# Second layer's long filters made during the first layer's merges and kept in DRAM; the step between the layers in two parts of the tokens

## The chip, the cores and the metric

One core of a Trainium2 chip. The time is that of one execution on the device in microseconds (us); the kernel before takes 2286.52 us, median of three runs (2286.14 to 2286.73). PE multiplies matrices, DVE works on vectors, ACT on activations and casts, POOL and SP also issue DMA transfers. All engines run their own instruction list in order and wait for each other by semaphores.

## The reference

Two layers over 128 context tokens and 512 latent tokens (640 columns, "T"), model width 1024. Each layer is one mixer with four branches from one input projection, gated, merged and projected:

```python
for l in range(DEPTH):                                   # DEPTH = 2
    shift, scale, gate = split(silu(cond) @ w_ada + b_ada, 3)
    h = rms_norm(x, norm_g) * (1.0 + scale) + shift
    u = h @ w_in                                          # 1024 -> 10752 columns in all
    ya = conformer_conv(...)  @ wo_conv                   # conv over 31 tokens
    filt = hyena_filters(L, ...)                          # depends on weights alone
    yb = hyena(u_proj, ..., filt, skip) @ wo_hyena        # long conv through FFT
    yc = multiscale_pool(...) @ wo_pool
    yd = block_attention(...) @ wo_attn
    gm = sigmoid(g_merge)                                 # one gate per branch
    merged = gm[0]*ya + gm[1]*yb + gm[2]*yc + gm[3]*yd
    x = x + gate * (merged @ w_out)
```

The filters come from a small network over the token position, are multiplied by a decay, normed and transformed (`spectra`); they need nothing of x.

## The kernel before

All matrices are held as a high and a low part of a 32-bit number, so a projection of 1024 rows into 128 columns over 640 tokens is, for each half j of 320 tokens, 16 matmuls with the high weights (`whi`) and 8 with the low (`wlo`), each 320 columns wide (`proj`, L386). A weight comes by a chain: SP loads `raw` (2 buffers), ACT casts `whi`, ACT writes −`whi` into `wlo`, POOL adds the original to it by an accumulating DMA (3 pairs of `whi`/`wlo`). Big data lie in 13 slots of SBUF (`sl`); projections use three PSUM banks (`mm`), small work three (`ax`), the transform one (`sc`).

The order on PE is planned when the program is built: `Loom` (L84) runs generators, its threads, each with a priority, and a thread yields the time from which it could go on; PE's order is what the planner chose. The other engines are ordered by the framework's scheduler, which follows what is ready and its priorities.

The stages of a layer: convolution stage with filters of the Hyena branch (`Hyena`, L839) and the branch's inputs, v/k/q, attention together with the Hyena branch's merge (`first`, written to `mscr`), the conformer's and pooling's inputs, then three merges of eight steps d each (attention, pooling, conformer; `merge`, L805), then `out_proj` (L1771): four blocks n of 256 output columns in token-major form, five tiles of 128 tokens, 24 matmuls each (`token_proj`, L418). Each block adds to the residual x, stores it (`store_x`), sums the squares of x and spawns `turned` (L752), which transposes x for the next layer and multiplies by 1 + scale. In between the chunks of w_ada for the next layer's shift and scale are done (`ada_chunk`, L603). After all four blocks `rms` (L712) makes the norm's factors from the sums, and `modulated` (L773) does, per 128 rows k of the eight: DVE's product with the factors (`u`), ACT's high part, DVE's low part. A projection of the next layer waits k by k on `a.ev[k]`.

A filter thread (`filters`, L872; one for each half q, four pieces c each) fetches decay (320 KB) and `hy_w` (64 KB) into the slot of the piece, casts the weights into `k` on ACT, does 10 matmuls `ax<-k,hd`, squares and sums, two tiny matmuls `ax<-ones`, and the transform: 8 matmuls into `sc`, 6 into `ax`, which DVE folds into the slot (`wx`, then `sl<-wx`). The second layer's eight pieces are spawned by `late_filters` (L1905) in the second block of out_proj (`ev_late`, L1779), so that they lie in out_proj, the step between the layers and the second layer's first projections.

Of the kernel before, what the change touches and what calls it, by code (L numbers as in the profile page):

```python
# [16 lines left out]
P = 128  # L17
# [215 lines left out]
def hybrid_flow_backbone(ctx: ExitStack, tc: tile.TileContext, i, o):  # L233
# [179 lines left out]
    def in_proj(l, c0, fn):  # L413
        w = yield from w_cols(l, c0)
        yield from both(w, 0, hT[0], 8, fn)
        wr.put(WD)

# [70 lines left out]
    scratch = tc.dram_tile([T, D], F32, name="xscratch")  # L488
    dve.memset(lnw, 1.0 / 512.0)
# [205 lines left out]
    def square_sum(xs, ssq, n):  # L695
        h, c0 = n // 2, 256 * (n % 2)
        for t in range(5):
# [14 lines left out]
    def rms(ssq):  # L712
        v = sm.tile([P, 5], F32, tag="rmsv", name=nm("rmsv"))
        rs = sm.tile([P, 5], F32, tag="rmsr", name=nm("rmsr"))
        dve.tensor_reduce(out=v, in_=ssq, axis=AX.X, op=ALU.add)
        dve.tensor_scalar(out=v, in0=v, scalar1=1.0 / D, scalar2=EPS, op0=ALU.mult, op1=ALU.add)
        rsqrt(rs, v, 5)
        return rs

    def modulated_first(a, xs, ssq):  # L720

        rs = rms(ssq)
        for h in range(2):
            xv = xs[h].v(0, 5, 512)
            for t in range(5):
                dve.tensor_scalar(out=xv[:, t, :], in0=xv[:, t, :], scalar1=rs[:, t:t + 1], scalar2=None,
                                  op0=ALU.mult)
        for h in range(2):
            xv = xs[h].v(0, 5, 512)
            yield lm.sync()  # L730
            pp = yield from ax.get()
            for c in range(4):
                pe.transpose(pp[:, 128 * c:128 * c + 128], xv[:, 0, 128 * c:128 * c + 128], ident)
            for c in range(4):
                k = 4 * h + c
                yield ev_mod[0][k // 2]
                ps = yield from mm.get()
                for t in range(4):
                    pe.transpose(ps[:, 128 * t:128 * t + 128], xv[:, 1 + t, 128 * c:128 * c + 128], ident)
                hf = yield from tr.get(T)  # L740
                A, S = mods[0][:, 1, k, :], mods[0][:, 0, k, :]
# [6 lines left out]
                a.ev[k].set()  # L748
            ax.put()
            xs[h].free()  # L750

    def turned(l, xs, xT, n, ev):  # L752
# [5 lines left out]
        for u in range(2):  # L758
# [3 lines left out]
            for t in range(4):  # L762
                pe.transpose(ps[:, 128 * t:128 * t + 128], xv[:, 1 + t, c], ident)
            A = mods[l][:, 1, 2 * n + u, :]
            act.activation(out=dst[:, 128:640], in_=ps, func=AF.Copy, scale=A[:, 1:2])
            mm.put()
            pp = yield from ax.get()
            pe.transpose(pp[:, 0:128], xv[:, 0, c], ident)
            act.activation(out=dst[:, 0:128], in_=pp[:, 0:128], func=AF.Copy, scale=A[:, 0:1])
            ax.put()  # L770
        ev.set()

    def modulated(l, a, xT, ssq, evs):  # L773

        rs = rms(ssq)
        yield lm.sync()
        row = yield from tr.get(T)
        ps = yield from mm.get()
        for t in range(1, 5):
            pe.transpose(ps[:, 128 * t - 128:128 * t], rs[:, t:t + 1].to_broadcast([P, P]), ident)  # L780
        act.copy(row[:, 128:640], ps)
        mm.put()
        pp = yield from ax.get()
        pe.transpose(pp[:, 0:128], rs[:, 0:1].to_broadcast([P, P]), ident)
        act.copy(row[:, 0:128], pp[:, 0:128])
        ax.put()
        for k in range(8):
            yield evs[k // 2]
            x = xT[k // 4].v((k % 4) * T, T)
            hf = yield from ur.get(T)  # L790
            S = mods[l][:, 0, k, :]
            dve.tensor_tensor(out=hf, in0=x, in1=row, op=ALU.mult)
            for c, t in ((1, slice(128, 640)), (0, slice(0, 128))):
                hi, lo, f = a.h(k)[:, t], a.l(k)[:, t], hf[:, t]
                act.activation(out=hi, in_=f, func=AF.Identity, bias=S[:, c:c + 1])
                dve.scalar_tensor_tensor(out=lo, in0=f, scalar=S[:, c:c + 1], in1=r32(hi),
                                         op0=ALU.add, op1=ALU.subtract)
            ur.put()
            a.ev[k].set()
            if k % 4 == 3:  # L800
                xT[k // 4].free()
# [37 lines left out]
    class Hyena:  # L839
# [32 lines left out]
        def filters(self, q):  # L872

            l = self.l
            if q == 0 and l > 0:
                s = yield from slot()
                self.tables(s)
# [27 lines left out]
            for c in range(4):  # L905
                if q == 0 and c not in self.flt:
# [3 lines left out]
                self.fetch(c, q)  # L910
                yield self.ld[c, q]
# [3 lines left out]
                if c < 3 and q == 0 and c + 1 not in self.flt and free and (self.gB or c < 1):  # L915
                    self.flt[c + 1] = Slot()
                if c + 1 in self.flt:
                    self.fetch(c + 1, q)
# [53 lines left out]
                self.ev_f[c, q].set()  # L972
            self.nf += 1
            if self.nf == 2:
                self.Bf.free()

# [47 lines left out]
        def inputs(self, c):  # L1024
# [4 lines left out]
            for u in range(3):  # L1029
# [4 lines left out]
                def take(j, ps):  # L1034
# [3 lines left out]
                    else:  # L1038
                        act.copy(pad[:, 322:642], ps)

                yield from in_proj(l, C_BP + 512 * u + 128 * c, take)
                uc = s.v(641 * u, 641)
                act.activation(out=uc, in_=pad[:, 1:642], func=AF.Identity,
                               scale=par(l, c, R_SW + 3 + u), bias=par(l, c, R_SB + u))
                for k in (0, 2):
                    dve.scalar_tensor_tensor(out=uc, in0=pad[:, k:k + 641],
                                             scalar=par(l, c, R_SW + 3 * k + u), in1=uc,
                                             op0=ALU.mult, op1=ALU.add)
                tr.put()
# [721 lines left out]
    def out_proj(l, ma, xs, ssq, rows, xT=None, evs=None):  # L1771
        for n in range(4):
# [6 lines left out]
            if n == 1:  # L1779
                ev_late[l].set()  # L1780
# [3 lines left out]
            def take(t0, ps):  # L1784
# [6 lines left out]
                tr.put()  # L1791

            yield from token_proj(i["w_out"][l][:, 256 * n:256 * n + 256], ma, take)
# [3 lines left out]
            else:  # L1797
                store_x(xs, scratch[0:LP], scratch[LP:T], n)
                square_sum(xs, ssq, n)
                lm.spawn(turned(l + 1, xs, xT, n, evs[n]), PT)  # L1800

    def layers():
# [3 lines left out]
        xT, evs = None, None  # L1806
        for l in range(DEPTH):
            hy = hys[l]
            a = yield from new_act(2)
            a.ev = [Event(lm) for _ in range(8)]  # L1810
            lm.spawn(modulated(l, a, xT, ssq, evs) if l else modulated_first(a, xs, ssq), PN)
# [10 lines left out]
            hy.gB = yield from slot()  # L1822
            at = Attention(l)
# [40 lines left out]
            yield from po.gated()  # L1864
            yield from merge(l, 2, po.pa, 4, i["wo_pool"][l], merged, "mid")
# [3 lines left out]
            ma = yield from new_act(2)  # L1869
# [12 lines left out]
            if l + 1 < DEPTH:  # L1882
                lm.spawn(late_filters(l + 1, ev_late[l]), 7)
                lm.spawn(ada_later([(1, j) for j in range(8, 12)], 0.0, GS), 50, LATA)
            if l + 1 < DEPTH:
                xT = yield from slots(2)
                evs = [Event(lm) for _ in range(4)]
            yield from out_proj(l, ma, xs, ssq, rows, xT, evs)
# [3 lines left out]
            if l + 1 < DEPTH:  # L1892
                yield evs[3]
# [11 lines left out]
    def late_filters(l, ev):  # L1905
        yield ev
        for q in range(2):
            hys[l].threads.append(lm.spawn(hys[l].filters(q), PF0))

# [4 lines left out]
    ev_late = [Event(lm) for _ in range(DEPTH)]  # L1914
# [153 lines left out]
```

## Time and profile before

| | before |
|---|---|
| runs | 2286.14, 2286.52, 2286.73 us |
| profiled execution | 2285.64 us, span 2283.8 us |
| mean granted clock of PE | 0.984 |
| PE busy | 2192.5 us (96%) |
| DVE, ACT, POOL busy | 58%, 52%, 26% |
| attention, pooling and conformer merges of the first layer, in the span | about 715 to 1085 us |
| out_proj and the step between the layers | about 1085 to 1220 us |
| second layer's convolution stage | from about 1220 us |

The profile is one execution; its span leaves out what lies before the first and after the last instruction. Where PE's window shows less than its length as busy, the difference is idle. PEclk is the granted clock as a share of 2.4 GHz.

### The profile page before, as it was taken

The numbers are of one execution on the slowest core, as the hardware profiler recorded it, in microseconds if no ns is written. First come the engines' busy times: TensorE is split into PE (matmuls) and PEld (weight loads), VectorE is DVE, ScalarE is ACT, GpSimd is POOL, SyncE is SP. The second block draws the span as 40 slices with busy tenths as digits, with TensorE's granted clock in tenths as the row PEclk, the third lists the DMA queues.
The fourth block names the chain that finished last, engine by engine and source line by source line (L and its number), as shares of the span: only waits on it lengthen the run. The fifth ranks groups of instructions, "written<-read, shape, count | busy, mean of one in ns | idle before, by whom it ended". The sixth has DMA issues, their size and how long they took to land.

```text
span 2283.8 us, 39935 instructions
## 1 busy us (share of the span) xinstructions
PE 2192.5 (96%) x15951; PEld 2145.5 (94%) x15951; DVE 1333.8 (58%) x2762; ACT 1190.4 (52%) x2169; POOL 590.2 (26%) x451
## 2 busy tenths in 40 slices
PE   5999999999999999999997999999999999999999
PEld 3899999999999999999987999999999999999999
DVE  5676786656679944122265777845766897522222
ACT  5544457667654335344564454656776543544442
POOL 2644321101112222222144353111111122222221
PEclk7899999999999999999998999999999999999999
DMA  9376766545568878899973656555455888698986
GB/s 280 104 159 143 163 141 122 101 79 104 109 126 146 151 123 151 150 168 167 226 185 73 109 106 123 105 101 98 82 109 102 150 150 150 113 164 148 173 169 137
DMA packets 508230, 311.83 MB, mean 137 GB/s; under 512 B 12760, under 2 KB 499352, under 8 KB 507789
## 3 DMA queue, kind: packets, MB, share of 16 engines
q0 software_dynamic: 223856, 122.96, 42.4%
q1 hardware_dynamic: 283476, 186.19, 27.3%
q8 instruction: 125, 2.05, 0.4%
q14 instruction: 60, 0.49, 0.1%
q10 hardware_dynamic: 713, 0.14, 0.0%
HBM read 297.02 MB, written 12.22 MB: 135 GB/s over the span
## 4 chain that ended last, share of the span: by engine, by line
PE 74%; issue 9%; DVE 8%; POOL 4%; ACT 3%; DMA 2%; ACTq 0%; SPq 0%; POOLq 0%; DVEq 0%
PE mm L193 58%; PE sc L193 6%; PE ax L193 6%; DVE sl L178 4%; PE ax L202 4%; POOL wlo L347 2%; POOL sl L178 1%; DMA sl<-in_hy_w_dram 1%; DMA wlo<-in_w_in_dram 1%; DVE wx L178 1%; DVE k L178 1%; ACT sl L178 0%; DVE t L178 0%; ACT u L178 0%; DVE u L178 0%
## 5 line engine op out<-in xcount | busy, mean ns | idle before, releaser
L193 PE MATMUL mm<-sl,whi 128*128 128x320 f32 x6304 | 1053.9, 312 | 9.6 <-DVE sl L178 3.9
L193 PEld LDWEIGHTS mm<-sl,whi 128*128 128x128 f32 x6304 | 948.1, 188 | 14.8 <-DVE sl L178 4.5
L193 PE MATMUL mm<-sl,wlo 128*128 128x320 f32 x3152 | 553.7, 311 | 0.9 <-DMA wlo<-in_w_in_dram 0.9
L347 POOL DMA_DIRECT2D wlo<-in_w_in_dram x173 | 264.9, 1531 | 860.2 <-ACT wlo L178 599.5
L193 PEld LDWEIGHTS mm<-sl,wlo 128*128 128x128 f32 x3152 | 483.3, 188 | 1.9 <-DMA wlo<-in_w_in_dram 1.1
L178 ACT CAST whi<-raw 128x1024 fp32r<-128x1024 f32 (+2 forms) x272 | 255.3, 939 | 436.3 <-PE mm L193 423.7
L178 DVE SCALAR_TENSOR_TENSOR t<-t,mm 128x320 f32<-128x320 f32 x192 | 93.2, 486 | 367.7 <-PE mm L193 306.3
L178 ACT ACTIVATE wlo<-whi 128x1024 fp32r<-128x1024 f32 (+2 forms) x269 | 254.9, 948 | 35.6 <-PE mm L193 32.7
L193 PE MATMUL mm<-whi,sl 128*128 128x256 f32 x1600 | 228.8, 286 | 4.2 <-ACT u L178 2.1
L178 DVE SCALAR_TENSOR_TENSOR sc<-sl,prm,sc 128x640 f32<-128x640 f32 (+14 forms) x232 | 207.3, 894 | 12.0 <-ACT sc L178 7.3
L193 PE MATMUL sc<-sl,sl 128*128 128x128 f32 (+1 forms) x1344 | 206.7, 297 | 7.9 <-DVE sl L178 4.2
L193 PEld LDWEIGHTS mm<-whi,sl 128*128 128x128 f32 x1600 | 205.9, 190 | 6.6 <-ACT u L178 2.3
L193 PEld LDWEIGHTS sc<-sl,sl 128*128 128x128 f32 x1344 | 182.3, 196 | 11.3 <-issue 5.5
L178 DVE TENSOR_TENSOR h<-ax,h 128x512 fp32r<-128x512 f32 (+1 forms) x200 | 120.3, 604 | 114.7 <-ACT h L178 113.0
L178 ACT ACTIVATE t<-mm 128x320 f32<-128x320 f32 x208 | 89.8, 432 | 145.9 <-PE mm L193 143.1
L178 DVE TENSOR_SCALAR_CACHE_REDUCE u<-sc,rq 128x640 f32<-128x640 f32 x128 | 112.6, 880 | 44.7 <-PE sc L193 43.8
L193 PE MATMUL mm<-wlo,sl 128*128 128x256 f32 x800 | 128.3, 283 | 5.5 <-DMA wlo<-in_w_in_dram 4.0
L178 ACT ACTIVATE u<-u,nb 128x640 f32<-128x640 f32 x128 | 106.2, 830 | 49.9 <-DVE u L178 49.3
L178 ACT CAST h<-ax 128x512 fp32r<-128x512 f32 (+1 forms) x200 | 102.5, 514 | 52.3 <-PE ax L202 49.9
L193 PE MATMUL ax<-h,sl 128*128 128x256 f32 (+1 forms) x656 | 121.7, 297 | 5.0 <-DVE h L178 3.8
L202 PE MATMUL ax<-ident,u 128*128 128x128 f32 x752 | 118.6, 273 | 3.6 <-DVE h L178 2.0
L193 PEld LDWEIGHTS mm<-wlo,sl 128*128 128x128 f32 x800 | 109.3, 190 | 6.3 <-DMA wlo<-in_w_in_dram 4.5
(213 smaller groups left out, 2232.9 us busy)
## 6 DMA issues: line engine op xcount, KB each, us to landing
raw<-in_w_in_dram SPq DMA_DIRECT2D x176, 512.0 KB
wlo<-in_w_in_dram POOLq DMA_DIRECT2D x173, 512.0 KB, 6.5
wlo<-in_w_ada_dram SPq DMA_DIRECT2D x19, 512.0 KB
whi<-in_w_ada_dram SPq DMA_DIRECT2D x19, 512.0 KB
raw<-in_wo_attn_dram SPq DMA_DIRECT2D x16, 512.0 KB
wlo<-in_wo_attn_dram POOLq DMA_DIRECT2D x16, 512.0 KB, 6.3
raw<-in_w_out_dram SPq DMA_DIRECT2D x16, 512.0 KB
wlo<-in_w_out_dram POOLq DMA_DIRECT2D x16, 512.0 KB, 7.2
```

What stands on the lines that cost most here:

```text
L178: r = f(*args, **kw)
L193: r = self.real.matmul(out, lhsT, rhs, **kw)
L202: r = self.real.transpose(out, in_, ident)
L347: nc.gpsimd.dma_start(out=lo[:, 0:w].rearrange("p (k c) -> p k c", k=kk), in_=src.bitcast(F32R), accum_op=ALU.add)
```

## The change

Three parts. First, the second layer's filters are spawned after `po.gated` of the first layer (between its attention and pooling merges) with a slot of their own, `fs`, in whose two halves the pieces of q = 0 and q = 1 follow on each other. A finished spectrum (128 × 1280 numbers, 640 KB) is stored to DRAM (`spec`), and the next piece is fetched into the same half; the planner counts at least 7.0 us from that point. A thread `spectra` loads them back in the second layer. Second, the last merge takes its output slots four steps at a time, and x is loaded after it (one half of it came earlier before). Third, the last block of out_proj goes by groups of token tiles, (0), (1, 2), (3, 4), each over all of k, so both its weight buffers are held to its end; squares, `turned`, `rms` and `modulated` go by two parts (tokens 0 to 383 and 384 to 639 of 640), events are `a.ev[j][k]`, and the second layer's first two projections go together, half by half (`in_pair`).

```diff
             if a.ev:
-                yield a.ev[ka]
+                yield a.ev[j][ka]
...
+    def in_pair(l, c0s, fns):
+        ws = []
+        for c0 in c0s:
+            ws.append((yield from w_cols(l, c0)))
+        for j in range(2):
+            for w, fn in zip(ws, fns):
+                ps = yield from mm.get()
+                yield from proj(ps[:, 0:320], w, 0, hT[0], [(k, k) for k in range(8)], j)
+                fn(j, ps[:, 0:320])
+                mm.put()
+        for _ in ws:
+            wr.put(WD)
+
+    def token_parts(src, a, fn):
+        ws = []
+        for kh in range(2):
+            ws.append((yield from weights(src[512 * kh:512 * kh + 512].rearrange("(k p) c -> p k c", p=P), 4, 256)))
+        for group in ((0,), (1, 2), (3, 4)):
+            ps = yield from mm.get()
+            for m, t in enumerate(group):
+                cols = slice(128 * t, 128 * t + 128)
+                for n, (part, i_w) in enumerate(((a.h, 0), (a.l, 0), (a.h, 1))):
+                    if m + n:
+                        yield
+                    for k in range(8):
+                        pe.matmul(ps[:, 256 * m:256 * m + 256], part(k)[:, cols], ws[k // 4][i_w][:, k % 4, :],
+                                  start=(m + n + k == 0), stop=(n == 2 and k == 7), skip_group_check=True)
...
+            mm.put()
+        for _ in ws:
+            wr.put(WD)
...
+    def modulated(l, a, xT, ssq, evs, evq):
+        row = yield from tr.get(T)
+        for j, t0, nt in ((0, 0, 3), (1, 3, 2)):
+            yield evq[j]
+            rs = rms(ssq[:, t0:t0 + nt])
...
+            for k in range(8):
+                yield evs[k // 2][j]
+                x = xT[k // 4].v((k % 4) * T, T)
+                hf = yield from ur.get(320)
...
+                dve.tensor_tensor(out=hf, in0=x[:, 320 * j:320 * j + 320], in1=row[:, 320 * j:320 * j + 320], op=ALU.mult)
...
+                a.ev[j][k].set()
...
         for d in range(8):
+            if mode == "last" and d % 4 == 0:
+                for part in (ma.hi, ma.lo):
+                    part.append((yield from slot(F32R)))
...
+            early = l > 0
+            if early and q == 0:
+                yield self.after
+                yield lambda: 0.0 if len(free) > 2 else INF
+                self.tables(Slot())
+                self.fs = Slot()
...
+                if early:
+                    self.flt[c] = self.fs
...
                 self.fetch(c, q)
+                if early:
+                    self.ld[c, q] = max(self.ld[c, q], lm.cur.t + 7.0)
...
                 yield from self.spectrum(ss, fb[:, :, 0], s.v(f0, 1280), True)
-                self.ev_f[c, q].set()
+                if early:
+                    sp.dma_start(out=spec[c, q], in_=s.v(f0, 1280))
+                else:
+                    self.ev_f[c, q].set()
...
+        def spectra(self):
+            yield lambda: 0.0 if self.nf == 2 else INF
+            for c in range(4):
+                yield lambda: 0.0 if c < 2 or c in self.bu else INF
+                self.flt[c] = yield from slot()
+                for q in range(2):
+                    self.ev_f[c, q].t = load(self.flt[c].v(1280 * q, 1280), spec[c, q])
...
-            if n == 1:
-                ev_late[l].set()
...
+                if split_:
+                    square_sum(xs, ssq, n, range(1 + t0, 1 + t0 + nt))
+                    if t0 >= 0:
+                        evq[t0 // 2].set()
+                        lm.spawn(turned(l + 1, xs, xT, n, evs, (t0 // 2,)), PT)
+            split_ = n == 3 and l + 1 < DEPTH
+            yield from (token_parts if split_ else token_proj)(i["w_out"][l][:, 256 * n:256 * n + 256], ma, take)
...
             yield from po.gated()
+            if l + 1 < DEPTH:
+                hys[l + 1].after = cv.ev_norm
+                for q in range(2):
+                    lm.spawn(hys[l + 1].filters(q), PF0 + q / 10)
...
-                lm.spawn(late_filters(l + 1, ev_late[l]), 7)
```

PE where the step between the layers ends, before: `ax<-whi,cs` are the matmuls of w_ada's chunks, `rmsr` the norm's factors, `k,hd` a filter piece.

```order
L202 MATMUL ax_12602<-ident,sl_11648 128x128
L193 MATMUL ax_12605<-whi_12515,cs 32x256 x4
L193 MATMUL ax_12605<-wlo_12517,cs 32x256 x4
L193 MATMUL ax_12644<-whi_12640,cs 32x256 x4
L193 MATMUL ax_12644<-wlo_12642,cs 32x256 x4
L202 MATMUL mm_12654<-ident,rmsr_12619 128x128 x4
L202 MATMUL ax_12660<-ident,rmsr_12619 128x128
L193 MATMUL ax_12707<-whi_12703,cs 32x256 x4
L193 MATMUL ax_12707<-wlo_12705,cs 32x256 x4
L193 MATMUL ax_12716<-ones,k_12553 128x1
L193 MATMUL ax_12716<-ones,sl_12188 128x1
L193 MATMUL ax_12724<-k_12597,hd_11995 128x256 x4
```

PE at the same place now: `mm<-ident,sl` of 2 are the transposes of one part of the tokens.

```order
L193 MATMUL ax_13010<-whi_13006,cs 32x256 x4
L193 MATMUL ax_13010<-wlo_13008,cs 32x256 x4
L202 MATMUL mm_13025<-ident,sl_12254 128x128 x2
L202 MATMUL ax_13032<-ident,sl_12254 128x128
L202 MATMUL mm_13045<-ident,sl_12254 128x128 x2
L202 MATMUL ax_13049<-ident,sl_12254 128x128
L193 MATMUL ax_13052<-whi_13035,cs 32x256 x4
L193 MATMUL ax_13052<-wlo_13037,cs 32x256 x4
L202 MATMUL mm_13073<-ident,sl_12254 128x128 x2
L202 MATMUL mm_13077<-ident,sl_12254 128x128 x2
L193 MATMUL ax_13088<-whi_13084,cs 32x256 x4
L193 MATMUL ax_13088<-wlo_13086,cs 32x256 x4
```

The filters' matmuls and their `ax<-ones` are gone from here; transposes by parts stand between three of the four chunks of w_ada, with the factors (`rmsr`, 3 tiles) nine rows further up, inside out_proj's last block.

SP in the pooling merge, before: loads of weights in turn, one of `w_in`, one of the merge's own.

```order
L342 DMA raw_10256<-in_w_in_dram 128x8x128
L342 DMA raw_10315<-in_wo_pool_dram 128x4x128
L342 DMA raw_10352<-in_w_in_dram 128x8x128
L342 DMA raw_10411<-in_wo_pool_dram 128x4x128
L342 DMA raw_10450<-in_w_in_dram 128x8x128
L342 DMA raw_10511<-in_conv_pw_dram 128x4x128
```

SP in the pooling merge now: `sl_9795` is the filters' slot, its halves stored and fetched again.

```order
L1031 DMA spec<-sl_9795 128x1280
L325 DMA sl_9795<-in_c_decay_dram 128x5x128
L325 DMA sl_9795<-in_hy_w_dram 64x2x128
L325 DMA sl_9795<-in_hy_b_dram 2x2x128
L1031 DMA spec<-sl_9795 128x1280
L342 DMA raw_10599<-in_wo_pool_dram 128x4x128
L325 DMA sl_9795<-in_c_decay_dram 128x5x128
L325 DMA sl_9795<-in_hy_w_dram 64x2x128
L325 DMA sl_9795<-in_hy_b_dram 2x2x128
L342 DMA raw_10668<-in_w_in_dram 128x8x128
L342 DMA raw_10761<-in_wo_pool_dram 128x4x128
```

Each fetch (three rows) stands behind the store of what its half held before; the second half's store stands behind the first's fetch, and weight loads behind that store and behind the second fetch.

ACT in the same merge, before: casts of weights (`whi`, `wlo`) and evictions (`t<-mm`) alone.

```order
L178 CAST whi_10161<-raw_10160 128x1024
L178 ACTIVATE wlo_10162<-whi_10161 128x1024
L178 ACTIVATE t_10063<-mm_10071 128x320
L178 CAST whi_10220<-raw_10219 128x512
L178 ACTIVATE wlo_10221<-whi_10220 128x512
L178 ACTIVATE t_10063<-mm_10097 128x320
L178 CAST whi_10257<-raw_10256 128x1024
L178 ACTIVATE wlo_10258<-whi_10257 128x1024
L178 ACTIVATE t_10159<-mm_10167 128x320
```

ACT there now: `k_10250`, `k_10258` and the copy into `sl_9795` belong to the fold of one half, `k_10319` are the casts of the weights fetched for the other.

```order
L178 CAST whi_10334<-raw_10333 128x1024
L178 ACTIVATE wlo_10335<-whi_10334 128x1024
L178 ACTIVATE t_10191<-mm_10199 128x320
L178 COPY k_10250<-sc_10238 128x512
L178 COPY sl_9795<-ax_10239 128x256
L178 COPY k_10258<-ax_10253 128x256
L178 CAST k_10319<-sl_9795 64x256 x2
L178 CAST k_10319<-sl_9795 66x256
L178 CAST whi_10456<-raw_10455 128x512
L178 ACTIVATE t_10191<-mm_10233 128x320
L178 ACTIVATE wlo_10457<-whi_10456 128x512
L178 CAST whi_10493<-raw_10492 128x1024
```

The casts `k_10319` stand ahead of the next weight's cast and ahead of the eviction of `mm_10233`.

## Rows read from the trace of the kernel before

**Rows 1.** Windows: a slice of the merges, the slice where out_proj begins; header names columns.
```profile
core 0: us, PE busy (x) PEld busy (x) DVE busy (x) ACT busy (x) POOL busy (x), PEclk, DMA share, GB/s
...
913.60:970.70 57.10, 57.10 (x390) 57.10 (x389) 9.01 (x15) 22.25 (x33) 14.68 (x11) 1.00 0.89 150
...
1084.90:1142.00 57.10, 54.62 (x427) 53.90 (x426) 13.91 (x23) 29.45 (x57) 10.30 (x8) 1.00 0.95 226
```

**Rows 2.** Windows of 10 us: the passage, and two of the next convolution stage.
```profile
1170.00:1180.00 10.00, 8.80 (x74) 8.20 (x74) 6.57 (x25) 9.04 (x24) 2.29 (x2) 1.00 0.58 173
1180.00:1190.00 10.00, 6.31 (x68) 3.70 (x67) 8.87 (x19) 8.30 (x20) 8.39 (x7) 0.94 1.00 234
1190.00:1200.00 10.00, 8.47 (x48) 8.21 (x47) 9.48 (x23) 7.68 (x15) 2.81 (x3) 0.72 1.08 174
1200.00:1210.00 10.00, 0.03 (x1) 0.03 (x1) 7.74 (x16) 4.21 (x10) 5.17 (x6) 0.62 0.27 78
1210.00:1220.00 10.00, 8.98 (x40) 8.69 (x41) 3.11 (x8) 1.92 (x4) 6.28 (x7) 0.53 0.01 4
...
1300.00:1310.00 10.00, 7.51 (x58) 7.04 (x58) 9.03 (x19) 4.07 (x7) 2.96 (x3) 1.00 0.62 106
1310.00:1320.00 10.00, 8.30 (x59) 7.84 (x58) 5.06 (x11) 3.40 (x10) 2.18 (x1) 1.00 0.73 133
```

**Rows 3.** Timeline of PE: two groups of 16 matmuls (start, duration, what).
```profile
1190.70 3.62 PE L193 MATMUL sc<-sl,sl 128*128 128x128 f32 x16
...
1225.92 1.95 PE L193 MATMUL sc<-sl,sl 128*128 128x128 f32 x16
```

**Rows 4.** Waits of PE, 1160 to 1225 (total, times, longest).
```profile
PE ax L193 <- ACT k L178: 11.5, 1, 11.5
```

**Rows 5.** Chain of work that ended last, 1163 to 1320 (start, duration, what).
```profile
1162.92 2.61 PE mm L193 x22
...
1168.76 0.51 ACT o L178 x2
...
1182.40 0.37 SPq L620
...
1182.87 5.32 DMA wlo<-in_w_ada_dram
...
1206.04 2.98 DMA sl<-in_hy_w_dram
...
1209.10 0.40 ACT k L178
...
1310.28 0.56 SPq L325
...
1310.89 6.48 DMA sl<-in_hy_w_dram
```

**Rows 6.** Timeline of DVE in the passage.
```profile
1165.56 0.69 DVE L178 TENSOR_TENSOR t<-mm,t 128x512 f32<-128x512 f32 x1 [1.33 <-PE mm L193]
...
1171.77 1.02 DVE L178 TENSOR_TENSOR wx<-k,sc 128x512 f32<-128x512 f32 x2 [3.04 <-ACT k L178]
...
1172.85 0.18 DVE L178 TENSOR_REDUCE rmsv<-ssq 128x5 f32<-128x20 f32 x1
...
1174.37 0.28 DVE L178 TENSOR_TENSOR wx<-ax,k 128x128 f32<-128x128 f32 x1
...
1175.16 1.28 DVE L178 TENSOR_TENSOR sl<-wx 128x512 f32<-128x512 f32 x2
...
1194.63 1.00 DVE L178 SCALAR_TENSOR_TENSOR sl<-u,mod,sl 128x512 fp32r<-128x512 f32 x2
```

**Rows 7.** Groups of instructions in the merges, 913.6 to 1084.9 (busy, mean ns).
```profile
L178 ACT CAST whi<-raw 128x512 fp32r<-128x512 f32 x17 | 10.5, 620 | 32.7 <-PE mm L193 32.7
...
L178 ACT ACTIVATE t<-mm 128x320 f32<-128x320 f32 x32 | 13.7, 430 | 24.4 <-PE mm L193 24.4
```

**Rows 8.** DMA issues in the merges (KB each, median us to landing).
```profile
wlo<-in_w_in_dram POOLq DMA_DIRECT2D x16, 512.0 KB, 6.6
```

More of the change, by code (lines that the diff above doesn't have):

```diff
@@ L693, in store_x, with square_sum @@
                      in_=v[:, 1:5, c0:c0 + 256])
-    def square_sum(xs, ssq, n):
+    def square_sum(xs, ssq, n, tiles=range(5)):
         h, c0 = n // 2, 256 * (n % 2)
-        for t in range(5):
+        for t in tiles:
             dump = op_.tile([P, 256], F32, tag="o", name=nm("o"))
@@ L761, in turned @@
             ps = yield from mm.get()
-            for t in range(4):
-                pe.transpose(ps[:, 128 * t:128 * t + 128], xv[:, 1 + t, c], ident)
+            tiles = [t for t in range(4) if t // 2 in parts]
+            for m, t in enumerate(tiles):
+                pe.transpose(ps[:, 128 * m:128 * m + 128], xv[:, 1 + t, c], ident)
             A = mods[l][:, 1, 2 * n + u, :]
-            act.activation(out=dst[:, 128:640], in_=ps, func=AF.Copy, scale=A[:, 1:2])
+            t0, w = 128 + 128 * tiles[0], 128 * len(tiles)
@@ L767, in turned @@
             pp = yield from ax.get()
-            pe.transpose(pp[:, 0:128], xv[:, 0, c], ident)
-            act.activation(out=dst[:, 0:128], in_=pp[:, 0:128], func=AF.Copy, scale=A[:, 0:1])
+            for t in range(nt):
+                pe.transpose(pp[:, 128 * t:128 * t + 128], rs[:, t:t + 1].to_broadcast([P, P]), ident)
+            act.copy(row[:, 128 * t0:128 * (t0 + nt)], pp[:, 0:128 * nt])
             ax.put()
[L771 to L801, printed above, removed]
@@ L914, in filters @@
                 dec = ss = s.v(f0, 5, 128)
[L915 to L918, printed above, removed]
+                if not early:
+                    if c < 3 and q == 0 and c + 1 not in self.flt and free and (self.gB or c < 1):
+                        self.flt[c + 1] = Slot()
+                    if c + 1 in self.flt:
+                        self.fetch(c + 1, q)
                 w0 = yield from kr.get(dt=F32R)
@@ L1028, in inputs, with padded @@
             s = self.bu[c]
-            for u in range(3):
+            def padded():
                 pad = yield from tr.get(643)
@@ L1039, in take @@
                         act.copy(pad[:, 322:642], ps)
[L1041 to L1049, printed above, removed]
+                return pad, take
+            for us in ((0, 1), (2,)) if l and c == 0 else ((0,), (1,), (2,)):
+                pads = []
+                for u in us:
+                    pads.append((yield from padded()))
+                c0s = [C_BP + 512 * u + 128 * c for u in us]
+                if len(us) == 2:
+                    yield from in_pair(l, c0s, [take for _, take in pads])
+                else:
+                    yield from in_proj(l, c0s[0], pads[0][1])
+                for u, (pad, _) in zip(us, pads):
+                    uc = s.v(641 * u, 641)
+                    act.activation(out=uc, in_=pad[:, 1:642], func=AF.Identity,
+                                   scale=par(l, c, R_SW + 3 + u), bias=par(l, c, R_SB + u))
+                    for k in (0, 2):
+                        dve.scalar_tensor_tensor(out=uc, in0=pad[:, k:k + 641],
+                                                 scalar=par(l, c, R_SW + 3 * k + u), in1=uc,
+                                                 op0=ALU.mult, op1=ALU.add)
+                    tr.put()
             self.ev_b[c].set()
@@ L1805, in layers @@
         lm.cur.t = ev_ssq.t
-        xT, evs = None, None
         for l in range(DEPTH):
             hy = hys[l]
-            a = yield from new_act(2)
-            a.ev = [Event(lm) for _ in range(8)]
-            lm.spawn(modulated(l, a, xT, ssq, evs) if l else modulated_first(a, xs, ssq), PN)
+            if l == 0:
+                a = yield from new_act(2)
+                a.ev = [[Event(lm) for _ in range(8)] for _ in range(2)]
+                lm.spawn(modulated_first(a, xs, ssq), PN)
             hT[0] = a
@@ L1886, in layers @@
                 xT = yield from slots(2)
-                evs = [Event(lm) for _ in range(4)]
-            yield from out_proj(l, ma, xs, ssq, rows, xT, evs)
+                evs = [[Event(lm) for _ in range(2)] for _ in range(4)]
+                evq = [Event(lm) for _ in range(2)]
+                a = yield from new_act(2)
+                a.ev = [[Event(lm) for _ in range(8)] for _ in range(2)]
+                lm.spawn(modulated(l + 1, a, xT, ssq, evs, evq), PN)
+                yield from out_proj(l, ma, xs, ssq, rows, xT, evs, evq)
+            else:
+                yield from out_proj(l, ma, xs, ssq, rows)
             for _ in range(2):
```

63 lines of the change are left out of this document (43 added, 20 removed).

## The prediction

> **What bounds the kernel now.** I read the windows by stage first. In the first layer's merges PE is busy 57.10 of 57.10 us at granted clock 1.00, while DVE needs 9.0 us, ACT 22.3 and POOL 14.7; only the DMA share is high, 0.89 [rows 1]. There PE is the bound and three engines have room. Then I read 10-us windows: from 1170 to 1220 PE idles 1.20, 3.69, 1.53, 9.97 and 1.02 us, 17.4 in all, and the granted clock falls to 0.72 and 0.53 where PE is busy for 8.47 and 8.98 us [rows 2]. At the lower level, 1.2 GHz, a group of 16 `sc` matmuls takes 3.62 us against 1.95 a little later at 2.4 GHz [rows 3]; half of the 17.45 busy us, 8.7, is lost that way. The passage between the layers costs 17.4 + 8.7 = 26.1 us. Two more dents: 2.49 + 1.70 = 4.2 us of idle in 1300–1320, in the second layer's convolution stage [rows 2], and 2.5 us in the slice where out_proj begins, 54.62 of 57.10 [rows 1].
>
> The waits name the worst: 11.5 us on ACT's `k`, a cast of filter weights [rows 4]. The chain of waits shows why: `k` waited for a fetch of `hy_w` of 2.98 us at 1206.04, issued only when DVE, filled with the passage's own multiplications and the filter's folding, let the slot go. The same thing at 1310.89 takes 6.48 us [rows 5].
>
> **Filters out of the passage and the convolution stage.** The filters' matmuls are moved, not saved: 8 pieces of 10 matmuls at 0.119 us and 14 at 0.12, some 23 us of PE work [rows 3, 5], go from the passage and the second layer's first projections into the merges, where they lie end to end as any other matmul. What goes is the waiting. In the convolution stage 4.2 us of idle hang on such fetches and on DVE; gates remain there, and I leave 1.2: **−3** (bounds 0 and −4.2).
>
> **Filters into the merges.** All pieces of one half q now live in one slot. Each goes: matmuls of `k,hd`, sums, 14 matmuls of 128 columns (`sc`, `ax`), folding, store of 640 KB, fetch of the next decay and weights (384 KB) into the same place, three casts, next `k,hd`. The order shows what PE does between the end of the 14 matmuls of one piece and the point where it needs the next one's casts: 78 matmuls of 320 columns and the other half's 14. In the merges a 320-column matmul takes 57.10/390 = 0.146 us [rows 1], one of 128 columns about 0.12 (1.95/16, [rows 3]): 11.4 + 1.7 = 13.1 us of cover. The chain beside it, from rows of the filter work before [rows 6]: folding 1.02 + 2 × 0.28 + an eviction of about 0.5 that stands between [rows 7] + 1.28 = 3.3; issue of the store 0.4; store S; issue of the weights behind the decay 0.6 [rows 5]; fetch F; three casts at 0.40 [rows 5]; then ACT's next rows in its order, a cast of `whi` at 0.62 and the eviction of `mm_10233` at 0.43 [rows 7], for whose bank PE waits. Without S and F that is 6.5, so the trip is free up to S + F = 13.1 − 6.5 = 6.6.
>
> F has two rows: 2.98 and 6.48. No row shows a 640 KB store. The nearest are two w_ada loads of 512 KB issued side by side, the second 5.32 us [rows 5], 1 MB in 5.8 us, which makes 640 KB 3.6 us at best; and POOL's 512 KB transfers in the merges, median 6.6 [rows 8], which makes 8.2. I take S = 5.3, the row nearest in size and kind, and F = 3.0: SP holds no raw load ahead of the fetch, since it stands blocked behind the store. Sum 8.3, which is 1.7 over. The second half's fetch comes behind the first's and its cover grows by the first's wait, so I charge one wait a step. Three steps (pieces 1 to 3): **+5.1**; bounds 0 (3.6 + 2.98) and 3 × 8.1 = +24 (8.2 + 6.48).
>
> The rest of the filter work in the merges costs nothing as long as DVE, ACT and POOL have the room of [rows 1]; folding and casts come to 2.9 us of DVE and 1.2 of ACT a piece [rows 5, 6]. If ACT were late, PE's three banks would fill within two projections; that is inside the upper bound. The reloads, 8 × 640 KB, are issued in the passage and after it, where the DMA share is 0.27 and 0.01 [rows 2]; each has long landed before the convolution stage, and their POOL and SP neighbours wait at most one landing. Nil.
>
> **Start of out_proj.** Both halves of x are now loaded at the end of the merge, behind the raw loads of w_out. Here 2.5 us are idle already [rows 1]; I take +0.5, bounds −2.5 (the later start of everything else leaves the loads time) and +4 (1.25 MB at the pace of the w_ada pair is 7 us, of which the first columns' work hides 3).
>
> **The passage in two parts.** PE's order after tiles 1 and 2 of the last column block, call that moment T0: 48 matmuls at 2.61/22 = 0.119 [rows 5], 5.7 us. On the chain: eviction 0.69 and an addition of the like, two squares with the reading of their sums at 0.51 [rows 5], 13 small DVE steps of 0.18 and a gap, at 1172.85 the first [rows 6], 2.7: 5.2 with the handing over about 5.4, so that the transposes of `rmsr`, which stand before PE's last 16 matmuls, hold PE by some 1.7. out_proj ends at T0 + 7.7. Only then are its two weight buffers free, and three pairs of w_ada buffers follow on each other: 3 × 5.3 [rows 5] puts the fourth ada chunk at T0 + 23.6 and the first projection at about T0 + 24.5. There the first token half is long modulated; the second follows at per k a multiplication, a cast and a subtraction for 320 columns, each about half of what 640 columns cost, 1.00 for the subtraction [rows 6], 1.4 us in all: its last k at T0 + 38 to 39. PE has 21.8 us of work until then (48 × 0.119, the transposes, four ada chunks, 96 matmuls of 320 columns). Lost: 38.5 − 21.8 = 16.7, and I add 1.3 for work at the lower clock that lies behind the chain: 18. Before 26.1: **−8.1**. Bounds: −15 (w_ada a pair in half the time, since they overlap in flight) and −2 (the clock stays low over all of both halves, as it did over 20 us before).
>
> **Sum.** Against the profiled execution of 2285.6 (span 2283.8 and 1.8 around it): −3 + 5.1 + 0.5 − 8.1 = −5.5, which is 2280.1. It lies 0.9 below the median of the runs, 2286.5; on that footing **2281.0**.
>
> **Rivals.** *The trip through DRAM is free.* S + F stays under 6.6, the merges stay at 57.1 of 57.1: 2281 − 5.1 = 2276. For it: 2.98 for the fetch, and 3.6 at best for the store. Against it: the DMA share of 0.89. By the Trainium skill ("DMA: Bandwidth & Descriptors", "Anatomy of one DMA — SWDGE (gpsimd) path") a transfer takes about 2 us plus bytes over 436 GB/s, which as an estimate makes S 3.5 and F 2.9, in all 6.4: this rival. The trace agrees at 2.98 and disagrees at 6.48, where others were in flight. Chance 0.13.
>
> *The trip at its busy price: slower.* In the merges store and fetch meet raw loads and POOL's accumulating transfers, S = 6.6 [rows 8] and F = 6.5 [rows 5]: 13.1, 6.5 over in each of three steps, +19.5 instead of +5.1: 2281 + 14 = 2295. It beats the gains of 8.1 and 3 as soon as 3 × (S + F − 6.6) exceeds 11, from S + F = 10.3. For it: the DMA share of 0.89, the 6.48 row. Against it: while SP stands blocked no raw load competes. The same page's section says that a transfer's engines do not wait for a semaphore, the issuing queue does; it speaks against the change. Here the order has it: raw loads stand behind each fetch, and no run shows yet what their lateness costs. Chance 0.23.
>
> *The passage is not shorter.* in_proj waits for w_ada, whose loads start only when out_proj lets its buffers go; the split only moves the wait. −2 in place of −8.1: 2287, no change. For it: PE's chain already went through a w_ada load at 1182.87 [rows 5], and there is less filter work left to fill the wait. Against it: the 11.5 us on `k` must go. Chance 0.24.
>
> **How the numbers follow.** The forecast has 0.40, with its own range 2272 to 2284 (S + F between 7.5 and 9.5, passage between −5 and −12). Measurement tells a change from none at about 0.2%, 4.6 us, here 2281.9 and 2291.1. Faster: the free trip 0.13, of the forecast 0.32, of the third rival 0.04: 0.49. Slower: of the busy trip 0.17, of the third rival 0.05: 0.22. The same: 0.08 of the forecast, 0.06 of the busy trip, 0.15 of the third rival, 0.29. Range: below, the free trip with the passage at −15 is 2269, and with a little from the start of out_proj 2267; above, the busy trip alone is 2295, with an unhelped passage 2301: I stop at 2297.
>
> **What would show it.** Right: in the windows of the passage PE's idle and low clock together about 18 us and no wait on ACT's `k`; in 1300–1320 little idle; in the merges three waits of 1 to 3 us, on ACT's `k` or on the eviction ahead of it. Free trip: none of them. Busy trip: SP's fetch of decay waits 6 us or more for its store, and PE idles 5 us or more at each. Third rival: PE's longest wait in the passage is on w_ada. Wrong altogether: idle in out_proj's first blocks, or PE waiting for `wlo` all along the merges.

## The result and the profile after

The changed kernel takes 2273.86 us (median of 4 runs, 2271.39 to 2274.85) against 2286.62 of the kernel before: ratio 0.9945, 95% interval 0.9931 to 0.9958, 12.8 us faster. The forecast was 2281.0, so the direction was right, the time lies in the range, and the gain is more than twice the one worked out. The range, 2267 to 2297, held no change and a loss as well, so that lying in it says little. The profiled execution of after is its fastest, 2271.39 us, so that the two traces differ by 14.3.

The windows of after, as in [rows 1] and [rows 2]: one row over the whole stretch of the merges that holds the filters, the slice from 1084.9, which is merges alone here (out_proj begins at 1143.8; in the trace before at 1099.6), ten-us slices of the passage, and the two in the convolution stage.

```profile
core 0: us, PE busy (x) PEld busy (x) DVE busy (x) ACT busy (x) POOL busy (x), PEclk, DMA share, GB/s
907.00:1143.00 236.00, 234.77 (x1666) 233.81 (x1665) 86.64 (x181) 111.81 (x191) 107.46 (x93) 1.00 0.82 158
1084.90:1142.00 57.10, 57.10 (x389) 57.10 (x388) 13.13 (x20) 26.27 (x38) 14.16 (x11) 1.00 0.87 153
1200.00:1210.00 10.00, 8.56 (x79) 8.01 (x82) 6.47 (x23) 3.94 (x13) 0.00 (x0) 1.00 0.22 67
1210.00:1220.00 10.00, 5.00 (x62) 1.93 (x50) 5.56 (x29) 7.75 (x19) 0.54 (x1) 0.99 1.01 327
1220.00:1230.00 10.00, 7.30 (x32) 5.69 (x33) 3.08 (x9) 5.33 (x15) 2.60 (x2) 0.67 1.05 230
1230.00:1240.00 10.00, 7.71 (x33) 7.45 (x32) 4.75 (x11) 4.40 (x13) 1.55 (x1) 0.67 1.26 247
1240.00:1250.00 10.00, 9.24 (x58) 8.46 (x58) 4.35 (x13) 7.54 (x12) 1.55 (x1) 0.99 0.77 209
1300.00:1310.00 10.00, 10.00 (x75) 10.00 (x75) 8.49 (x16) 3.60 (x5) 5.59 (x4) 1.00 0.76 199
1310.00:1320.00 10.00, 10.00 (x76) 10.00 (x76) 6.22 (x14) 4.27 (x9) 1.57 (x1) 1.00 0.75 121
```

The merges hold the filters at 234.77 of 236 us busy. Where 1300–1320 had 4.2 us of idle there is none, and none in the whole convolution stage (1258 to 1377; before it idled 4.5 us from 1217 to 1383). The passage idles 1.4, 5.0, 2.7, 2.3 and 0.8 us, 12.2 where it was 17.4, and the granted clock falls to 0.67 over two slices. The waits of PE over out_proj, passage and convolution stage (total, times, longest), to be read beside [rows 4]:

```profile
PE mm L193 <- DMA wlo<-in_w_in_dram: 4.9, 2, 2.6
PE ax L193 <- DMA wlo<-in_w_ada_dram: 3.8, 3, 2.3
PE ax L202 <- DVE rmsr L178: 1.4, 1, 1.4
PE ax L193 <- DMA whi<-in_w_ada_dram: 1.3, 2, 0.9
```

The 11.5 us on `k` are gone. Ten of the twelve us of idle are now waits for weights: w_ada and the `wlo` of the first two w_in weights.

To put both kernels and all experiments on one scale I took from each trace, for every two neighbouring matmuls, the distance of their starts, less the usual distance for such a pair (the lower fifth of all pairs of the same two kinds in the two traces), and summed by stage. That counts idle time, lower clock and small delays together. "Merges" are the stretch from the pooling merge to out_proj (906 to 1099 before, 907 to 1143 after), "passage" is the 50 us from out_proj's end, "norm" the 50 us about the conformer's norm ahead of the pooling merge, "rest" all other stages, which the change doesn't touch. A row is one execution: those of the kernel that stores twice and of the step of 10 us lie 4.3 and 5.2 us above the median of their runs, so they show where time is lost better than how much.

| lost by PE, us | norm | merges | out_proj | passage | conv. stage | rest | all |
|---|---|---|---|---|---|---|---|
| before | 3.2 | 2.7 | 4.8 | 25.5 | 10.4 | 151.7 | 198.3 |
| after | 5.8 | 6.7 | 2.0 | 20.4 | 2.1 | 148.0 | 185.0 |
| difference | +2.6 | +4.0 | −2.8 | −5.1 | −8.3 | −3.7 | −13.3 |
| forecast | 0 | +5.1 | +0.5 | −8.1 | −3 | 0 | −5.5 |
| filters only | 5.4 | 6.6 | 2.0 | 21.5 | 2.1 | 153.6 | 191.2 |
| parts only | 3.2 | 4.0 | 5.5 | 15.4 | 16.9 | 147.4 | 192.4 |
| gate chunks early | 6.9 | 5.9 | 1.8 | 8.9 | 1.8 | 149.6 | 174.9 |
| the same, one part | 5.1 | 4.6 | 1.6 | 19.8 | 2.0 | 147.3 | 180.4 |
| before, chunks early | 3.0 | 2.5 | 5.4 | 26.5 | 16.8 | 146.1 | 200.3 |
| gate chunks late | 7.6 | 7.6 | 2.0 | 9.7 | 5.7 | 152.0 | 184.6 |
| stored twice | 7.3 | 23.8 | 2.0 | 20.2 | 2.1 | 151.8 | 207.2 |
| early, step 4 us | 10.6 | 18.4 | 1.8 | 9.3 | 1.8 | 146.2 | 188.1 |
| early, step 10 us | 5.9 | 13.2 | 1.8 | 9.6 | 1.8 | 151.7 | 184.0 |

The rest moves by some us from execution to execution and with the plan, 146 to 154, and no cause of it is claimed. One thing ahead of the prediction has to be put right: the w_ada chunks that lie in the passage are not those of the next layer's shift and scale, which are made early in the first layer, but the four of its gates, needed only in the second layer's out_proj. Nothing in the passage needs them.

### The profile page after: what moved, and what is told of

The parts are those of the page before. It is cut to its first block, busy times and chain, and to the rows that moved or that the text cites. A ratio compares the mean times of both kernels' runs of the same rounds, so it can differ in the third digit from the quotient of the medians.

```text
span 2269.6 us, 40007 instructions
## 1 busy us (share of the span) xinstructions
PE 2189.7 (96%) x15951; PEld 2140.5 (94%) x15951; DVE 1329.2 (59%) x2791; ACT 1190.8 (52%) x2179; POOL 585.5 (26%) x451
## 5 line engine op out<-in xcount | busy, mean ns | idle before, releaser
L193 PE MATMUL mm<-sl,whi 128*128 128x320 f32 x6304 | 1059.1, 313 | 10.6 <-DVE t L178 3.2
```

The costliest lines, as they stand in the source:

```text
L193: r = self.real.matmul(out, lhsT, rhs, **kw)
```

## Experiments

Nine kernels, each profiled and timed in five rounds beside the kernel before (2285.5 to 2286.4 in these jobs).

**Filters only: early filters, passage in one part.** The edits give `modulated` and `turned` back their form of before, wait for the factors once, and drop `in_pair`:

```diff
-            split_ = n == 3 and l + 1 < DEPTH
+            split_ = False
...
-            for us in ((0, 1), (2,)) if l and c == 0 else ((0,), (1,), (2,)):
+            for us in ((0,), (1,), (2,)):
```

> The filters lie in the first layer's merges as in the changed kernel, but the passage is in one part again (last block of out_proj, squares, factors and modulation for all 640 tokens, the next layer's first projections one after the other). Theory: the passage gained from both parts of the change, so about half of its 6.7 us comes back: about 2278 us against 2274, with the convolution stage (no idle) and the start of out_proj as in the changed kernel. Rival 1, the split alone shortened the passage: 2280.5 or more. Rival 2, the filters' leaving alone shortened it: within 2 us of 2274.

Measured 2274.72 us, ratio 0.9952 (0.9939 to 0.9964), against 0.9945 with the split: the second rival. The split is worth 1.1 us in the passage (21.5 against 20.4), within what runs differ by. What it does can be seen in the waits, first of this run, then of the changed kernel above:

```profile
PE mm L202 <- DVE t L178: 6.2, 1, 6.2
PE ax L202 <- ACT sl L178: 2.1, 1, 2.1
PE mm L193 <- ACT sl L178: 2.0, 2, 1.1
...
PE ax L193 <- DMA wlo<-in_w_ada_dram: 0.3, 1, 0.3
```

In one part PE waits 6.2 us for the norm's factors and next to nothing (0.3) for w_ada; in two parts 1.4 us for the factors and 5.1 for w_ada. One wait was changed for the other.

**Parts only: two-part passage, filters where they were.**

```diff
-                hys[l + 1].after = cv.ev_norm
-                for q in range(2):
-                    lm.spawn(hys[l + 1].filters(q), PF0 + q / 10)
+                pass
...
+                lm.spawn(late_filters(l + 1, ev_late[l]), 7)
```

> The passage is in two parts as in the changed kernel, but the second layer's filters lie where they were before (spawned in out_proj's second block, no store to DRAM), and x and the last merge's slots as before. Theory: the convolution stage keeps its idle (4 us in two windows of 10), the start of out_proj its 2.5 us, and the passage gains some 3: about 2283 us against 2286.6 of the kernel before. Rival 1, the split alone shortened the passage: 2280. Rival 2, the split does nothing: 2286 to 2287.

Measured 2278.27, ratio 0.9965 (0.9952 to 0.9977): 7 us faster alone, a little more than the first rival's 6.6. Its passage is short, 15.4, but the convolution stage grows to 16.9; both together go from 35.9 to 32.3, 3.6 us, near the 3 of the theory, and the rest of the 7 is in other stages. The filters' waits were pushed on, not removed: in the convolution stage PE waits 8.2 us where it waited 4.5. In one thing this passage differs from that of the changed kernel: `modulated` starts after out_proj here, so that PE meets the first factors (`rmsr`) at 1175.8, 5 us behind out_proj's end and not inside its last block. With early filters the two stages are at 23.6 without and 22.5 with the split.

**Gate chunks early.** The changed kernel with the second layer's gate chunks made in the first layer's attention stage:

```diff
-                jobs = [(0, j) for j in range(8, 12)] + [(1, j) for j in range(8)]
+                jobs = [(0, j) for j in range(8, 12)] + [(1, j) for j in range(12)]
...
-            if l + 1 < DEPTH:
-                lm.spawn(ada_later([(1, j) for j in range(8, 12)], 0.0, GS), 50, LATA)
```

> The changed kernel with the second layer's four gate chunks of w_ada (its 3 MB... of which the passage shows 5.0 us of PE's waits) made in the first layer's attention stage, after the eight of shift and scale, and not in the passage. Theory: they hold PE in the passage, and their loads hold the first weights of the next layer; without them 2274 becomes about 2268. Rival: the wait only moves to the next thing, the modulation of the second part or the first wlo of w_in: 2272 to 2274, with as much idle in 1200 to 1250.

Measured 2261.92 (2260.65 to 2264.56), ratio 0.9899 (0.9885 to 0.9912), more than the theory asked and the fastest of all. The windows over the passage's 50 us, before, changed kernel and this one (columns as above):

```profile
1167.00:1217.00 50.00, 32.59 (x243) 28.08 (x243) 37.50 (x93) 33.09 (x75) 24.23 (x21) 0.79 0.63 145
```

```profile
1208.00:1258.00 50.00, 39.26 (x254) 33.19 (x253) 21.98 (x73) 32.04 (x67) 8.72 (x6) 0.86 1.06 249
```

```profile
1211.00:1261.00 50.00, 45.86 (x297) 43.08 (x296) 30.82 (x90) 36.25 (x77) 13.33 (x9) 0.97 0.87 185
```

PE is busy 45.9 of 50 us where it was 39.3 and, before, 32.6, and the mean granted clock is 0.97, against 0.86 and 0.79. Its waits on weights are gone, those that are left are the chain that the prediction followed:

```profile
PE mm L202 <- ACT sl L178: 2.2, 3, 0.8
PE ax L202 <- DVE rmsr L178: 1.5, 1, 1.5
PE mm L193 <- ACT sl L178: 1.4, 2, 0.8
```

**The same with the passage in one part** (both edits).

> Filters in the merges, gate chunks of w_ada in the first layer's attention stage, and the passage in one part. Beside the run with the gate chunks early and the passage in two parts (2261.9) it shows what the two parts are worth once no w_ada load stands in the passage. Theory: the split's gain was eaten by w_ada loads that wait for the last block's two weight buffers; without the chunks it comes out, so this kernel stays 6 us or more behind, 2268 to 2271. Rival: the split is worth nothing in either setting: within 2 us of 2262.

Measured 2271.05, ratio 0.9941 (0.9927 to 0.9954): 9 us behind, as the theory said. The passage loses 19.8 against 8.9, and the row that does most of it is the wait for the factors:

```profile
1212.08 1.09 PE L202 MATMUL mm<-ident,rmsr 128*128 128x128 f32 x4 [5.98 <-DVE t L178]
```

So the split is worth 11 us of the passage (9 of the time) where no w_ada load stands in it, and 1 where one does.

**The kernel before with the gate chunks early** (the first edit above and the spawn taken out, nothing else).

> The kernel before with nothing changed but the four gate chunks made in the first layer's attention stage. Theory: its passage hangs on the filters (11.5 us on k) and w_ada adds 2 to 3 us of waits, so 2286 becomes 2282 to 2284. Rival: w_ada was the bound before as well, and the chunks alone give the whole of what they give in the changed kernel: 2274 or so.

Measured 2290.18, ratio 1.0014 (1.0006 to 1.0023): no gain, rather 3 to 4 us more. Theory and rival both fell, though the reason of the theory stands: w_ada did not bound the old passage. With its four chunks gone the filters' own waits came in their place (passage 26.5 against 25.5, convolution stage 16.8 against 10.4), on POOL and DVE:

```profile
PE ax L193 <- POOL sl L178: 3.8, 1, 3.8
PE ax L193 <- DVE sl L178: 3.1, 1, 3.1
PE mm L193 <- DVE sl L178: 2.9, 3, 2.2
PE ax L193 <- DVE wx L178: 2.7, 1, 2.7
```

**Gate chunks late**, behind the passage:

```diff
-                lm.spawn(ada_later([(1, j) for j in range(8, 12)], 0.0, GS), 50, LATA)
+                lm.spawn(ada_later([(1, j) for j in range(8, 12)], 14.0, 120.0), 5, LATA)
```

> The changed kernel with the four gate chunks put behind the passage, into the second layer's convolution stage; the first layer's attention stage stays as it was. Theory: it is the chunks' place in the passage that cost, not where they went, so the passage is as short as with the chunks early: about 2264. Rival: the gain of that run came from its attention stage, re-planned with the chunks in it (its loss before the merges was some 4 us smaller): 2270 or more.

Measured 2275.18, ratio 0.9953 (0.9941 to 0.9966), no faster than the changed kernel. The theory had the passage right (9.7), and the time is the rival's: 3.6 us came back in the convolution stage, where the chunks now stand, and some more in norm, merges and the rest (152.0 against 148.0). Whether that last part is the plan of the second layer's attention or its scatter stays open. The place to which the chunks go counts as much as that they go.

**Stored twice.**

```diff
                     sp.dma_start(out=spec[c, q], in_=s.v(f0, 1280))
+                    sp.dma_start(out=spec2[c, q], in_=s.v(f0, 1280))
```

> The changed kernel with each finished spectrum stored twice, to two places, so that the fetch into the same half waits for both; PE's order is the same. Theory: the trip through DRAM fills its cover (15.2 us of PE's work, 0.2 us over at the first fetch), so each of three steps is lengthened by the second store, some 3 to 5 us: +9 to +15, about 2286 us. Rival, the trip has slack: within 2 us of 2274.

Measured 2289.32, ratio 1.0015 (1.0006 to 1.0024): +15.5 on the changed kernel, just past the upper end of the theory. The merges lose 23.8 against 6.7. Of these 17 us more, 9 are waits (10.3 against 1.2), and most of the other 8 lies in the matmuls behind them, at a lower granted clock. The waits, and the longest of the three on ACT's `k` in the timeline of PE:

```profile
PE ax L193 <- ACT k L178: 8.4, 3, 4.3
PE ax L193 <- DVE k L178: 1.9, 4, 0.6
```

```profile
960.50 2.52 PE L193 MATMUL mm<-sl,whi 128*128 128x320 f32 x16
967.28 0.38 PE L193 MATMUL ax<-k,hd 128*128 128x256 f32 x1 [4.26 <-ACT k L178]
968.22 2.29 PE L193 MATMUL ax<-k,hd 66*128 66x256 f32 x9 [0.56 <-DVE k L178]
970.31 2.33 PE L193 MATMUL mm<-sl,wlo 128*128 128x320 f32 x8
972.44 2.21 PE L193 MATMUL mm<-sl,whi 128*128 128x320 f32 x8
974.50 0.75 PE L193 MATMUL mm<-sl,wlo 128*128 128x320 f32 x4
```

After the wait of 4.26 us eight `wlo` matmuls take 2.33 us, where the granted clock is 0.50 (968.3 to 973.0), 1.2 GHz; further on, four take 0.75, the usual pace.

**Gate chunks early, with the planner's 7 us at 10 and at 4.**

```diff
-                    self.ld[c, q] = max(self.ld[c, q], lm.cur.t + 7.0)
+                    self.ld[c, q] = max(self.ld[c, q], lm.cur.t + 10.0)
```

> Gate chunks early as above, and the planner counts 10 us instead of 7 for a spectrum's store and the next fetch, so more of PE's work lies between two pieces of a half. Theory: what is left of the trip's price are waits of 1 to 1.5 us in all on k, so 1 to 2 us less than 2261.9. Rival: the merges' extra loss is no wait at all but PE's matmuls being a little further apart: no change within 1 us.

> Gate chunks early as before, and the planner counts 4 us instead of 7 for a store and the next fetch. In PE's order 64 to 78 matmuls of 320 columns stand between one fold and the second half's next k,hd where 84 to 88 stood, some 18 fewer, 2.6 us of cover a step. Theory: at 7 us the trip just fills its cover, so three steps lose 2.6 us each and a little more by the clock: 2268 to 2272 against 2261.9, with waits on ACT's k of 2 to 3 us each in the merges. Rival: the cover is ample and the wide step lost for another reason: within 2 us of 2262.

At 10 us 2270.45, ratio 0.9931 (0.9918 to 0.9943); at 4 us 2277.75, ratio 0.9968 (0.9955 to 0.9980); both slower than 2261.92 with 7. The narrow step went as its theory said and beyond: the merges lose 18.4 against 5.9, the waits on ACT's `k` are 6.0 us in three:

```profile
PE ax L193 <- ACT k L178: 6.0, 3, 3.6
```

The wide step answered to neither expectation: 13.2 us lost in the merges, some 6 of them in waits on `t`, `k` and a `wlo` of w_in. The planner laid the pieces against the weights in another way; which of its choices did that was not tried.

## Why the prediction was right, and where its sizes were off

The direction was right, and the sign of every term but that of out_proj; the size, 12.8 us for 5.5, was not. The convolution stage gave nearly three times its term, out_proj gained where a loss was added, the trip cost less than its term, and the passage gained mostly by another cause than the one worked out. That a forecast with these errors lies in the right direction is in part luck.

**The trip through DRAM** (+5.1 forecast; the merges lose 4.0 more than before). Most of the 4.0 is not the trip. All of PE's waits in the merges of after, from 0.15 us up:

```profile
PE ax L193 <- DVE k L178: 1.0, 2, 0.8
PE mm L193 <- ACT t L178: 0.2, 1, 0.2
```

In the six trips PE waits 0.82 us once and 0.17 once, where three waits of 1 to 3 us were named as the sign; the remaining 0.17 stands before the first trip. By the table's measure the trips cost some 1.9 us, the first piece 0.5, and 16 places where PE goes back from a filter's small matmuls to a projection's 1.4 in all: the second matmul there starts 0.23 us after the first instead of 0.145. The prediction put these at nothing ("end to end as any other matmul"). The nearness of 5.1 and 4.0 is luck. The timeline of after at the first trip (start, duration, what, wait):

```profile
937.97 1.50 PE L193 MATMUL ax<-sl,sl 128*128 128x128 f32 x12
...
940.79 1.29 DVE L178 TENSOR_TENSOR sl<-wx 128x512 f32<-128x512 f32 x2
...
942.11 0.34 SPq L1031 DMA_DIRECT2D spec<-sl  x1
...
947.83 0.57 SPq L325 DMA_DIRECT2D sl<-in_c_decay_dram  x1
...
952.54 1.25 ACT L178 CAST k<-sl 64x256 fp32r<-64x256 f32 x3 [4.07 <-DMA sl<-in_hy_w_dram]
...
954.70 1.14 PE L193 MATMUL mm<-sl,whi 128*128 128x320 f32 x6 [0.17 <-ACT t L178]
```

The store is issued at 942.11; SP can issue the decay load at 947.83, so S is 5.7 us (5.3 taken); the weights of the fetch, issued at 948.45, release the casts at 952.54, so F is 4.1 (3.0 taken). S + F is 9.8, more than the 8.3 of the sum, and the rest of the chain 5.4 (6.5 taken). But PE's transform matmuls ahead of it end at 939.5, and it waits only from 954.5 for 0.17 us: its cover was 15.1 us and not 13.1. A transform's 8 rows of `sc` and 6 of `ax` are x16 and x12 in the trace, two instructions for each, which a look at [rows 3] would have shown: the cover was the mis-sized figure, by 2.0, and the price by 0.4, the other way round. So the trip just fits, which is what the free rival said of the time, though not by its condition: S + F is not under 6.6. The store written twice and the narrow step show that there is no slack behind it. The busy rival was not far: with the second store the change is a loss, 2289 against 2285.5.

**The price of a transfer.** The rule of the Trainium skill ("DMA: Bandwidth & Descriptors", "Anatomy of one DMA — SWDGE (gpsimd) path") gave S 3.5 and F 2.9 as an estimate; that section is on transfers issued by way of gpsimd, and these are issued by SP. The trace has 5.7 and 4.1 in the merges, where others were in flight. The measurement decides; by the rule's figures the trip would have had some 3 us of slack, and it had none.

**The convolution stage** (−3 forecast, −8.3 measured). The step took the idle of two windows of 10 us for the whole loss. They hold 4.2 of the stage's 4.5 us of idle, and of the 1.2 that were to remain nothing did. The other 5.9 of the 10.4 were left out: 1.4 in the stage's first 10 us, at a granted clock of 0.88, and small delays all along it. With the filters gone it loses 2.1, in every kernel that has them early and the gate chunks elsewhere.

**Start of out_proj** (+0.5 forecast, −2.8 measured). The step counted the x loads that come later and left out what goes: the loads of the filters' tables (1280 KB) and of decay, issued there before at 1095 to 1103. All early-filter kernels lose 1.6 to 2.0 us there, all late-filter ones 4.8 to 5.5. As late filters and the earlier x load go together in these kernels, which of them it was is not separated.

**The passage** (−8.1 forecast, −5.1 measured, and for another reason). The sum followed the split's chain and gave its gain to the split. The first links of the chain came about as worked out: `rmsr` held PE 1.44 us (1.7 forecast), the fourth chunk ended 20 us after T0 (23.6). Its end did not bind: PE waited 0.8 us for rows of the second part, since weights held it until then. Of the 5.1 us, 4.0 are the filters' leaving (21.5 with one part) and 1.1 the split; taken the other way round, the split alone takes 10.1 from the passage and gives 6.5 of it back in the convolution stage. The third rival named the mechanism, w_ada loads that start only when out_proj lets its buffers go, and the runs with the chunks moved show what it cost: 20.4 to 8.9 and 9.7. (In the changed kernel the loads of three of the four chunks are issued from 1207.0 on; out_proj's last matmul ends at 1208.4.) It was wrong in the time, since the 11.5 us on `k` did go. In the sum, idle was too large, 16.7 against 12.1 from T0 on, and the work at the lower clock far too small, 1.3 against most of 9.7 (20.4 less the idle 10.7). What it left out was the `wlo` of the first two w_in weights, 4.9 us behind those loads.

The second of these two took 16.3 us from its issue at 1220.35 to its landing; with the gate chunks early the first two took 8.8 and 8.1. Two spectra of 640 KB were fetched back beside it, issued from 1221.54 on, and the prediction put these reloads at nil. No run moves them, so what share of the wait is theirs stays open.

**The norm** (nothing forecast, +2.6). The first filter pieces join DVE's work there, and PE waits 1.57 us on DVE's `t` where it waited 0.41; in some executions the clock falls behind a wait of 2.08 us that both kernels have.

Some 4 us of the difference between the two profiled executions lie in stages that the change does not touch.

## What to carry to other kernels

Work that fills a stage's idle engine can be what makes it idle: before a chain is shortened, ask of every load in that stage whether anything there needs it, and move what does not; here that was worth nearly as much as the whole change (11.9 and 12.8 us), but only to a place with room: moved late, the same chunks gave nothing. A round trip through memory is free up to the work that the order puts beside it, so count that work in the instructions of the trace and not in rows of the program. And gains of two edits in one stage do not add: each was worth 7 to 11 us alone, both together 13, and the second came out in full only when the next wait had been removed.

## What the hardware showed that was not expected

Some waits of PE in the merges cost more than their length. In the kernel that stores twice, waits of 4.26, 1.88 and 2.27 us were each followed by matmuls at half pace and a granted clock of 0.50, the level of 1.2 GHz (eight `wlo` matmuls 2.33 us against 1.34); the same followed 1.80 and 3.60 us with the narrow step and 2.03 us with the wide one (eight `whi` in 2.33). Behind waits of 1.70 us (wide step), 1.04 us (parts only) and 0.82 us (after) the clock stayed at 1.00. With the second store 9 us more of waits went with 17 us more lost. It is no fixed rule: the wait of 2.08 us at the conformer's norm is the same in both kernels, but the windows around it (first the kernel before, then the changed one) show the granted clock at 1.00 in the one and at 0.90 and 0.93 in the other, where 16 `whi` matmuls after it take 3.97 us against 2.52.

```profile
850.00:860.00 10.00, 7.92 (x56) 1.00 0.61 106
860.00:870.00 10.00, 9.70 (x66) 1.00 0.66 116
```

```profile
850.00:860.00 10.00, 7.92 (x52) 0.90 1.01 245
860.00:870.00 10.00, 9.70 (x61) 0.93 0.55 136
```
